# Borders between the stages of a two-layer diffusion block: order of the modulation rows, PSUM banks, and where two attention groups wait

## The chip, the core and the metric

The kernel runs on one NeuronCore of a Trainium2 chip. The metric is the device time of one execution in microseconds, the median of several runs. The engines are named as the profile names them: PE (TensorE; PEld is its weight load), DVE (VectorE), ACT (ScalarE), POOL (GpSimd), SP (SyncE, which issues nearly all DMAs here). Each engine takes its instructions in program order and waits at the head of its own queue for semaphores of others. PSUM has eight banks of 128 x 512 fp32.

## What is computed

Two transformer layers over 512 latent tokens (x) and 256 context tokens (ctx), width 1024. Every normalised input is scaled and shifted by modulation rows that come from a conditioning vector, `silu(c) @ ada_w`: nine rows of 1024 for each layer and stream. Shortened from the reference:

```python
for i in range(2):
    mx = (silu(c) @ ada_w[i] + ada_b[i]).reshape(B, 9, 1, D)      # of x
    mc = (silu(c_ctx) @ ada_w[i] + ada_b[i]).reshape(9, D)        # of ctx
    fx = swiglu(pre(hx, norm_w[i, 0], mx[:, 0], mx[:, 1]), w_gate[i, 0], w_up[i, 0], w_down[i, 0])
    hx = hx + 0.5 * mx[:, 2] * fx                                 # the same for hc
    ax, ac = pre(hx, norm_w[i, 1], mx[:, 3], mx[:, 4]), pre(hc, norm_w[i, 1], mc[3], mc[4])
    ox, oc = gqa_window(ax, ac) if i == 0 else diff_attn(ax, ac)  # each ends in "@ w_out"
    hx = hx + mx[:, 5] * ox
    fx = swiglu(pre(hx, norm_w[i, 2], mx[:, 6], mx[:, 7]), w_gate[i, 1], w_up[i, 1], w_down[i, 1])
    hx = hx + 0.5 * mx[:, 8] * fx
return rmsnorm(hx, final_norm_w)                                   # pre(h, w, shift, scale) = rmsnorm(h, w) * (1 + scale) + shift
```

## The kernel before

**Layout and stages.** Activations are kept transposed: the 1024 channels are 8 blocks `d` of 128 partitions, the 768 tokens (256 ctx, then 512 x) lie along the free dimension. `hT` (128 x 8 x 768) is the residual stream. `run` goes through six stages: `ffn(0,0)`, `gqa`, `ffn(0,1)`, `ffn(1,0)`, `diff`, `ffn(1,1)`; the last needs x alone.

**fp32 by three products.** Every operand is split into a rounded part and a rest. `weights` loads a 128 x 1024 weight tile into `w_raw` (a ring of four buffers), casts it on ACT into `w_hi` (L55) and subtracts on POOL into `w_lo` (L56; two buffers each). A product is then three matmuls: hi by hi, hi by lo, lo by hi.

**Ending a stage.** The last projection of a stage makes block `d` after block `d` of 128 channels in PSUM. As each is done, `residual` (DVE, L302) adds it to `hT`, once for ctx (256 columns) and once for x (512). The callback `after(d)` is then `x_block`: ACT writes the scaled copy `xh` (L184), DVE the rest `xl` (L185), ACT squares (`sq`, L194 and L197), and POOL adds the squares up in `acc` (L199; DVE for the last block). That makes the next stage's input while PE still projects.

**Starting a stage.** `ffn` opens the pool `pbig` of four double-bank tiles called `big` and projects the first gate and up blocks at once (`project_k`, L257): for each k of the 8 channel blocks six matmuls, k by k, so that block k of `xh` and `xl` is needed only at step k. The norm factor is applied afterwards. `projected` copies two bias columns from PSUM (DVE, L262). The attentions start in the same way with `project_halves` (L276), in two single-bank tiles.

**Modulation rows.** A `side` list of `ada_block`s (load a 128 x 1024 tile into `w_raw`, multiply it on DVE by the conditioning vector with an accumulating L131, once per stream) is worked off by `more()`: one block in each `up_block` and some in the down-projection. They feed a later stage. Their `ada_junk` output has one buffer.

**What sets the order.** The code is traced once; a scheduler then places each instruction on its engine's queue as soon as its inputs look ready, so code that is written later can stand earlier in a queue. A pool of tiles hands out its buffers in a ring; where a pool is opened over memory that another one had, each new tile waits for the last users of just the tiles that lay there.

**Attention outputs.** In `gqa`, `values(g, pp, qb)` makes the output of group g (of 4) and query block qb (of 6), 128 x 2 x 128. It is split into `oh` (ACT, L482) and the rest `o1` (POOL, L483) and both are written to the DRAM tensor `od` (in the profile `god`, L484 and L485). `load_o` reads a group back as `og` (L491). Groups 0 and 1 go through the first half of the out-projection while groups 2 and 3 are still attended to (`out_proj(0, ...)`); `out_proj(1, ...)` is the second half, with `after`. `diff` does the same with eight heads: heads 0 to 3 first, then `out_proj(1, ...)` over heads 4 to 7 (`o4` to `o7`, L727 to L729), whose last one never leaves the chip. `out_proj` takes units of two blocks; for the units (0, 1) it first adds up the groups or heads that are ready and then the late ones.

## Time and profile before

| | |
|---|---|
| median of 3 runs | 2881.77 us (2878.62 to 2882.25) |
| the profiled execution, own time | 2884.58 us |
| its span from the first to the last instruction | 2882.8 us |
| PE busy | 2765.0 us (96%) |
| PEld / DVE / POOL / ACT busy | 90% / 53% / 44% / 33% |
| mean granted TensorE clock | 0.988 of full |
| HBM | 275.63 MB, 96 GB/s over the span |

PE is busy for all but 118 us of the span. So a number that matters for the end is one in which PE waits, or in which it runs at a lower clock: the granted clock stands at 1.0 or at 0.5 (2.4 or 1.2 GHz), and the mean over a stretch tells what part of it was at half. A timeline row gives start and duration in us, engine, line, operation, output and inputs, shape, how many like it were merged, and in brackets how long the engine had been idle just before and who released it.

### The profile page before, as it was taken

The page shows a single profiled execution, that of the slowest core. Times are in us where ns is not written, and L with a number is a line of the kernel's source. Part 1 is how long each engine was busy: PE and PEld are TensorE (multiplying, and loading weights), DVE is VectorE, ACT ScalarE, POOL GpSimd, SP SyncE. Part 2 cuts the span into 40 slices and gives each one's busy share as a digit, 9 for nine tenths or more (in the row PEclk, how much of TensorE's full clock was granted, in tenths as well). Part 3 has the DMA queues.
Part 4 walks back from the last instruction along what each step waited for, and adds up shares of the span by engine and source line. Part 5 has one row for each costly group of instructions (what it writes and reads, how often), then busy time and mean ns, then how long its engine had stood idle before and what let it go on. Part 6 is the DMA issues. An engine that isn't in the chain of part 4 may idle for free. (4 is left out here: it accounts for less than half of the span.)

```text
span 2882.8 us, 40921 instructions
## 1 busy us (share of the span) xinstructions
PE 2765.0 (96%) x16162; PEld 2583.7 (90%) x16162; DVE 1523.9 (53%) x2661; ACT 962.3 (33%) x1727; POOL 1274.4 (44%) x750
## 2 busy tenths in 40 slices
...
GB/s 277 104 126 100 134 123 95 113 146 90 65 135 112 81 75 116 81 92 121 88 81 103 77 118 87 86 121 93 82 94 77 88 93 111 88 91 100 103 103 45
DMA packets 113567, 296.38 MB, mean 103 GB/s; under 512 B 13024, under 2 KB 31072, under 8 KB 113376
## 3 DMA queue, kind: packets, MB, share of 16 engines
...
q8 instruction: 128, 2.10, 0.3%
...
## 5 line engine op out<-in xcount | busy, mean ns | idle before, releaser
L56 POOL TENSOR_TENSOR w_lo<-w_raw,w_hi 128x1024 fp32r<-128x1024 f32 (+2 forms) x377 | 799.8, 2122 | 1114.2 <-ACT w_hi L55 1091.7
L55 ACT CAST w_hi<-w_raw 128x1024 fp32r<-128x1024 f32 (+2 forms) x377 | 337.5, 895 | 1142.4 <-PE big L70 398.1
L257 PE MATMUL big<-xh,w_hi 128*128 128x384 f32 (+3 forms) x2816 | 691.9, 327 | 22.4 <-DVE hT L302 13.1
L257 PE MATMUL big<-xl,w_hi 128*128 128x384 f32 (+3 forms) x2816 | 689.4, 326 | 3.3 <-DVE xl L185 3.2
L257 PE MATMUL big<-xh,w_lo 128*128 128x384 f32 (+3 forms) x2816 | 690.9, 327 | 0.4 <-POOL w_lo L56 0.4
L257 PEld LDWEIGHTS big<-xh,w_hi 128*128 128x128 f32 x2816 | 501.0, 191 | 26.7 <-ACT sq L197 11.1
L257 PEld LDWEIGHTS big<-xl,w_hi 128*128 128x128 f32 x2816 | 498.7, 190 | 4.1 <-DVE xl L185 4.1
L257 PEld LDWEIGHTS big<-xh,w_lo 128*128 128x128 f32 x2816 | 496.9, 190 | 0.8 <-POOL w_lo L56 0.8
L131 DVE SCALAR_TENSOR_TENSOR ada_junk<-w_raw,s_bc 128x1024 f32<-128x1024 f32 x224 | 330.1, 1474 | 304.5 <-DMA w_raw<-ada_w 302.3
L262 DVE COPY bias<-big 128x2 f32<-128x2 f32 x176 | 27.7, 158 | 629.3 <-PE big L257 629.2
L68 PE MATMUL big<-hh,w_hi 128*128 128x512 f32 (+1 forms) x1200 | 327.6, 344 | 0.0
L70 PE MATMUL big<-hl,w_hi 128*128 128x512 f32 (+1 forms) x1200 | 326.9, 343 | 0.0
L72 PE MATMUL big<-hh,w_lo 128*128 128x512 f32 (+1 forms) x1200 | 326.8, 344 | 0.0
L302 DVE SCALAR_TENSOR_TENSOR hT<-big,mod,hT 128x512 f32<-128x512 f32 (+1 forms) x288 | 167.9, 618 | 179.4 <-PE big L72 179.0
L70 PEld LDWEIGHTS big<-hl,w_hi 128*128 128x128 f32 x1200 | 225.6, 188 | 30.1
L72 PEld LDWEIGHTS big<-hh,w_lo 128*128 128x128 f32 x1200 | 224.7, 188 | 28.8 <-POOL w_lo L56 0.2
L68 PEld LDWEIGHTS big<-hh,w_hi 128*128 128x128 f32 x1200 | 224.8, 188 | 27.4
L969 POOL TENSOR_TENSOR hl<-tb,hh 128x768 fp32r<-128x768 f32 (+1 forms) x88 | 151.3, 1719 | 171.8 <-ACT hh L968 170.6
L964 DVE SCALAR_TENSOR_TENSOR tb<-tb,bias,ta 128x512 f32<-128x512 f32 (+1 forms) x154 | 176.2, 1177 | 8.3 <-DVE tb L295 0.5
L276 PE MATMUL half<-xh,w_hi 128*128 128x384 f32 (+3 forms) x464 | 154.6, 333 | 21.0 <-DVE ta L288 19.1
L968 ACT CAST hh<-tb 128x768 fp32r<-128x768 f32 (+1 forms) x88 | 68.7, 781 | 268.2 <-DVE tb L964 268.1
L276 PE MATMUL half<-xl,w_hi 128*128 128x384 f32 (+3 forms) x464 | 153.1, 330 | 0.0
...
## 6 DMA issues: line engine op xcount, KB each, us to landing
w_raw<-ffn_gu SPq DMA_DIRECT2D x176, 512.0 KB, 3.3
w_raw<-ada_w SPq DMA_DIRECT2D x128, 512.0 KB, 3.3
...
w_raw<-diff_in SPq DMA_DIRECT2D x24, 512.0 KB, 3.3
w_raw<-gqa_in SPq DMA_DIRECT2D x12, 512.0 KB, 3.5
...
ada_raw<-ada_w SPq DMA_DIRECT2D x8, 512.0 KB, 9.4
```

The source lines that it names most:

```text
L55: nc.scalar.copy(out=hi[:, :cols], in_=raw[:, :cols])
L56: nc.gpsimd.tensor_tensor(out=lo[:, :cols], in0=raw[:, :cols], in1=hi[:, :cols].bitcast(F32), op=ALU.subtract)
L68: nc.tensor.matmul(o, wh, xh, start=(k == 0), stop=False)
L70: nc.tensor.matmul(o, wh, xl, start=False, stop=False)
L72: nc.tensor.matmul(o, wl, xh, start=False, stop=(k == n - 1))
L131: getattr(nc, engines[s]).scalar_tensor_tensor(out=junk, in0=raw, scalar=1.0, in1=self.sbc[:, s], op0=ALU.mult, op1=ALU.mult, accum_out=se ...
L257: mm(ps[:, c, :e - s], w[:, k], x[:, k, s:e], start=first, stop=last)
L276: mm(ps[:, :e - s], w_[:, k], x[:, k, s:e], start=(k == 0 and i == 0), stop=(k == ND - 1 and i == 2))
L302: self.nc.vector.scalar_tensor_tensor(out=h, in0=o, scalar=self.mv(l, s, c, d), in1=h, op0=ALU.mult, op1=ALU.add)
L964: nc.vector.scalar_tensor_tensor(out=u[:, tk], in0=u[:, tk], scalar=bu[:, s:s + 1], in1=g[:, tk], op0=ALU.add, op1=ALU.mult)
L968: nc.scalar.copy(out=hh[:, toks], in_=u[:, toks])
L969: nc.gpsimd.tensor_tensor(out=hl[:, toks], in0=u[:, toks], in1=hh[:, toks].bitcast(F32), op=ALU.subtract)
```

## The change

Three things are changed, all of them where one stage ends and the next begins.

- **Modulation rows.** `projected` keeps the bias copy (L262) as `bias_copy`. While the index of the current block is 0, that is in the first `up_block` of the three `ffn` after the first one, `more()` runs inside `issue_after(self.bias_copy)`: what the `ada_block` puts on DVE is queued behind that copy, so behind the end of the first projection. Later blocks follow, since `ada_junk` has one buffer. DMAs on SP are not bound by it. `ffn(1,1)` has no such rows, so two stages are touched: `ffn(0,1)` and `ffn(1,0)`.
- **PSUM banks.** The out-projections of `gqa` and `diff` take some blocks from a pool `pfirst` of two banks which lies lowest (`gqa`: blocks 0 and 4, `diff`: blocks 0 and 1) and the rest from six banks; and `diff` opens its pools in the opposite order. In the built program the first `big` tile of `ffn(0,1)` has banks 0 and 1. Before, bank 0 was block 4's and bank 1 the 512 x tokens of block 7, the last one; now both were block 4's. The first tile of `diff` had bank 4, which the last block of `ffn(1,0)` had; now it has bank 0, block 4's, and its second half bank 3, block 6's. The first `big` tile of `ffn(1,1)` had bank 0 of block 6 and bank 1 of block 5; now blocks 0 and 1.
- **Groups 2 and 3 of `gqa`.** Their outputs are written straight into on-chip tiles: group 2 into `og2`, group 3 into four buffers of the query ring `qs` that are free by then. 24 stores, 8 loads and the DRAM space of two groups are gone. The split of a group 3 output is two ACT copies and two POOL subtractions of 128 x 128 in place of one each of 128 x 256. The pool `gqa_q` is opened earlier, so that it can be released later.

```diff
@@ -259,7 +259,7 @@
     def projected(self, ps, xonly=False):
         n = 256 if xonly else 384
         bias = self.sp.tile([P, 2], F32, name="bias")
-        self.nc.vector.tensor_copy(out=bias, in_=ps[:, 1, n:n + 2])
+        self.bias_copy = self.nc.vector.tensor_copy(out=bias, in_=ps[:, 1, n:n + 2]).ins
         return ps[:, :, :n], bias
 
     def project_halves(self, src, xonly=False, pool=None, tag="half"):
...
         sinks = lp.tile([P, 16], F32, name="sinks")
         nsink = lp.tile([P, 16], F32, name="nsink")
-        od = self.dp.tile([4, 2, P, 2, T], F32, name="god")
+        od = self.dp.tile([2, 2, P, 2, T], F32, name="god")
         self.hp.release()
         o2p = self.sb("gqa_o2", 1)
+        rq = self.sb("gqa_q", 8)
         rpp = self.sb("gqa_p", 8)
         rp = self.sb("gqa_r", 2)
         rt = self.sb("gqa_t", 3)
         rk = self.sb("gqa_k", 3)
-        rq = self.sb("gqa_q", 8)
         self.pbig = self.ps("pgqa", 1)
         ptr = self.ps("pgqa_t", 2)
...
             nc.vector.tensor_tensor(out=o1[0:64], in0=av[0:64, 0:256], in1=o2[0:64], op=ALU.add)
             nc.vector.tensor_tensor(out=o1[64:128], in0=av[64:128, 256:512], in1=o2[64:128], op=ALU.add)
             qc = slice(CTX + qb * P, CTX + (qb + 1) * P) if qb < 4 else slice((qb - 4) * P, (qb - 3) * P)
-            oh = rp.tile([P, 256], F32R, name="oh")
-            nc.scalar.copy(out=oh, in_=o1)
-            nc.gpsimd.tensor_tensor(out=o1, in0=o1, in1=oh.bitcast(F32), op=ALU.subtract)
-            nc.sync.dma_start(od[g, 0][:, :, qc], oh.bitcast(F32).rearrange("p (c n) -> p c n", c=2))
-            nc.sync.dma_start(od[g, 1][:, :, qc], o1.rearrange("p (c n) -> p c n", c=2))
+            o1 = o1.rearrange("p (c n) -> p c n", c=2)
+            if g < 2:
+                oh = rp.tile([P, 2, P], F32R, name="oh")
+                nc.scalar.copy(out=oh, in_=o1)
+                nc.gpsimd.tensor_tensor(out=o1, in0=o1, in1=oh.bitcast(F32), op=ALU.subtract)
+                nc.sync.dma_start(od[g, 0][:, :, qc], oh.bitcast(F32))
+                nc.sync.dma_start(od[g, 1][:, :, qc], o1)
+            elif g == 2:
+                oh = o2t[:, 0, :, qc]
+                nc.scalar.copy(out=oh, in_=o1)
+                nc.gpsimd.tensor_tensor(out=o2t[:, 1, :, qc], in0=o1, in1=oh.bitcast(F32), op=ALU.subtract)
+            else:
+                for c in range(2):
+                    oh = o3t[c][:, qc]
+                    nc.scalar.copy(out=oh, in_=o1[:, c])
+                    nc.gpsimd.tensor_tensor(out=o3t[2 + c][:, qc], in0=o1[:, c], in1=oh.bitcast(F32), op=ALU.subtract)
 
         def load_o(pool, g):
             t = pool.tile([P, 2, 2, T], F32R, name=f"og{g}")
-            for tk in (slice(0, T),) if g < 3 else (slice(CTX, 512), slice(512, T), CT):
-                for c in range(2):
-                    nc.sync.dma_start(t[:, c, :, tk].bitcast(F32), od[g, c][:, :, tk])
-            return t
...
-        def out_proj(pr, os_, units, after=None):
+            for c in range(2):
+                nc.sync.dma_start(t[:, c].bitcast(F32), od[g, c])
+            return part(t)
+
+        def part(t):
+
+            return lambda c, r: t[:, c, r]
+
+        def out_proj(pr, os_, units, after=None, first_banks=None):
 
             mm = nc.tensor.matmul
             cuts = ((1, CT), (0, XT))
@@ -499,7 +513,8 @@
             for u in units:
                 w = self.weights(a["gqa_out"][pr, u])
                 for i in range(2):
-                    todo.append((u * 2 + i, i, w, [self.pbig.tile([P, 512], F32, name="half")[:, :tk.stop - tk.start]
+                    pool = first_banks if first_banks and u * 2 + i in (0, 4) else self.pbig
+                    todo.append((u * 2 + i, i, w, [pool.tile([P, 512], F32, name="half")[:, :tk.stop - tk.start]
                                                    for s, tk in cuts]))
             for part in (((0, 1, 2, 3),) if len(units) == 1 else ((0, 1), (2, 3))):
...
@@ -508,12 +523,14 @@
                         for w, c, first, last in ((wh, 0, r == 0, False), (wh, 1, False, False),
                                                   (wl, 0, False, r == 3)):
                             for ps, (s, tk) in zip(outs, cuts):
-                                mm(ps, w[:, i * 4 + r], o[:, c, r % 2, tk], start=first, stop=last)
+                                mm(ps, w[:, i * 4 + r], o(c, r % 2)[:, tk], start=first, stop=last)
                     if part[-1] == 3:
                         self.residual(outs, cuts, 0, 5, d)
                         if after:
                             after(d)
...
                 o01 = self.sb("gqa_o", 1, side="right")
                 os_ = [load_o(o01, 0), load_o(o01, 1)]
-                o2 = load_o(o2p, 2)
+
+                o3t = [rq.tile([P, T], F32R, name="qs") for _ in range(4)]
             nxt = step(i + 1) if i < 23 else None
             other(i)
             values(g, pp, qb)
             pp = nxt
         o01.release()
-        rq.release(); rk.release(); rt.release(); rp.release(); rpp.release()
+        rk.release(); rt.release(); rp.release(); rpp.release()
         pss.release(); pav.release(); ptr.release(); self.pbig.release()
-        o3p = self.sb("gqa_o3", 1)
-        os_ = [o2, load_o(o3p, 3)]
+        os_ = [part(o2t), lambda c, r: o3t[2 * c + r]]
         self.x_open()
         self.x_bias(0, 2)
-        self.pbig = self.ps("pgqa_o", 8)
-        out_proj(1, os_, (0, 1), after)
-        for u in (2, 3):
-            out_proj(1, os_, (u,), after)
-        self.pbig.release()
-        o3p.release(); o2p.release()
+
+        pfirst = self.ps("pgqa_f", 2)
+        self.pbig = self.ps("pgqa_o", 6)
+        for units in ((0, 1), (2,), (3,)):
+            out_proj(1, os_, units, after, pfirst)
+        self.pbig.release(); pfirst.release()
+        rq.release(); o2p.release()
         lp.release()
 
 
     def diff(self, after):
         nc, a = self.nc, self.a
-        self.pbig = self.ps("pdiff", 1)
+        pss = self.ps("pdiff_s", 4)
         ptr = self.ps("pdiff_t", 2)
         pav = self.ps("pdiff_v", 1)
-        pss = self.ps("pdiff_s", 4)
+        self.pbig = self.ps("pdiff", 1)
         lp = self.sb("diff", 1)
         kp = self.sb("diff_k", 4)
...
@@ -713,13 +731,14 @@
                 nc.sync.dma_start(od[h, 0], oh.bitcast(F32))
                 nc.sync.dma_start(flat(od[h, 1]), r0)
 
-        def out_proj(pr, os_, units, pool, tag, after=None):
+        def out_proj(pr, os_, units, pool, tag, after=None, first_banks=None):
 
             mm = nc.tensor.matmul
             todo = []
             for u in units:
                 w = self.weights(a["diff_out"][pr, u])
-                todo += [(u * 2 + i, i, w, pool.tile([P, 512], F32, name=tag)) for i in range(2)]
+                todo += [(u * 2 + i, i, w, (first_banks if first_banks and u == 0 else pool).tile([P, 512], F32, name=tag))
+                         for i in range(2)]
             for part in (((0, 1, 2, 3),) if len(units) == 1 else ((0, 1, 2), (3,))):
                 for d, i, (wh, wl), ps in todo:
...
@@ -754,9 +773,10 @@
             if h < 7:
                 ks, qs, vv = new["k"], new["q"], new["v"]
         op.release(); vp.release(); pp.release(); p1p.release(); kp.release()
-        pss.release(); pav.release(); ptr.release(); self.pbig.release()
+        self.pbig.release(); pav.release(); ptr.release(); pss.release()
 
         op = self.sb("diff_oall", 1)
+        pfirst = self.ps("pdiff_f", 2)
         po = self.ps("pdiff_o", 6)
         self.x_bias(1, 2, True)
...
             os_.append((o[:, 0], o[:, 1]))
         os_.append((o7[:, 0], o7[:, 1]))
         for units in ((0, 1), (2,), (3,)):
-            out_proj(1, os_, units, po, "o", after)
-        po.release()
+            out_proj(1, os_, units, po, "o", after, pfirst)
+        po.release(); pfirst.release()
         op.release()
         lp.release()
...
         todo = list(side)
 
         def more(n=1):
-            for _ in range(n):
-                if todo:
-                    self.ada_block(self.adap, *todo.pop(0))
+
+            with self.tc.issue_after(self.bias_copy) if i == 0 and not first else nullcontext():
+                for _ in range(n):
+                    if todo:
+                        self.ada_block(self.adap, *todo.pop(0))
 
         if first:
```

The DVE queue at the border from `gqa` to `ffn(0,1)`, before, for the last block: its residuals `hT`, its rests `xl`, and what stands between them and the first two bias copies.

```order
L302 SCALAR_TENSOR_TENSOR hT<-half,mod,hT 128x256
L302 SCALAR_TENSOR_TENSOR hT<-half,mod,hT 128x512
L185 SCALAR_TENSOR_TENSOR xl<-hT,mod,xh 128x256
L185 SCALAR_TENSOR_TENSOR xl<-hT,mod,xh 128x512
L131 SCALAR_TENSOR_TENSOR ada_junk,mod<-w_raw,s_bc 128x1024
L199 TENSOR_TENSOR acc<-sq,acc 128x768
L131 SCALAR_TENSOR_TENSOR ada_junk,mod<-w_raw,s_bc 128x1024
L262 COPY bias<-big 128x2 x2
```

Two of the six modulation rows `ada_junk` stand ahead of the bias copies here; the other four stand higher up, among the rests of the blocks before. The same stretch now:

```order
L302 SCALAR_TENSOR_TENSOR hT<-half,mod,hT 128x256
L302 SCALAR_TENSOR_TENSOR hT<-half,mod,hT 128x512
L185 SCALAR_TENSOR_TENSOR xl<-hT,mod,xh 128x256
L185 SCALAR_TENSOR_TENSOR xl<-hT,mod,xh 128x512
L199 TENSOR_TENSOR acc<-sq,acc 128x768
L262 COPY bias<-big 128x2
L131 SCALAR_TENSOR_TENSOR ada_junk,mod<-w_raw,s_bc 128x1024 x5
L262 COPY bias<-big 128x2
L131 SCALAR_TENSOR_TENSOR ada_junk,mod<-w_raw,s_bc 128x1024
L210 TENSOR_SCALAR tb<-big 128x768
```

The six rows ahead of the first bias copy are behind it: five between the two bias copies, one after the second, ahead of the norm factor (`tb`, `rstd`). At the border from `ffn(0,1)` to `ffn(1,0)` it is the same with its six rows.

The SP queue at the end of `gqa` before, `og_8655` being group 3 and `og_7822` group 2:

```order
L485 DMA god<-o_8464 256x1x128
L491 DMA og_8655<-god 128x2x256 x3
L484 DMA god<-oh 256x1x128
L491 DMA og_8655<-god 128x2x256
L485 DMA god<-o_8597 256x1x128
L120 DMA s_bc<-cond 128x1024 x2
L484 DMA god<-oh 256x1x128
L485 DMA god<-o_8631 256x1x128
L491 DMA og_8655<-god 128x2x256 x2
L126 DMA w_raw<-ada_w 128x1024
```

Six loads and the last five stores of group 3 stand ahead of the first load of a modulation row (`ada_w`) here. And now, from the last load of group 1 on:

```order
L501 DMA og_7802<-god 128x1536 x2
L54 DMA w_raw<-gqa_out 128x1024 x2
L54 DMA w_raw<-ffn_gu 128x1024 x2
L120 DMA s_bc<-cond 128x1024 x2
L126 DMA w_raw<-ada_w 128x1024
```

The loads and stores of groups 2 and 3 are gone; the weight loads are next to each other.

The PE queue at the end of `diff`, before: the value products `av` of the last head, its sum of squares (L699) and then the first out-projection products of heads 4 to 6 (`o_21694` is head 4).

```order
L691 MATMUL av<-pth,vl 128x512
L692 MATMUL av<-ptl,vh 128x512
L690 MATMUL av<-pth,vh 128x512
L691 MATMUL av<-pth,vl 128x512
L692 MATMUL av<-ptl,vh 128x512
L699 MATMUL tr<-acc,ones 128x512
L727 MATMUL o<-o_21694,w_hi 128x512
L728 MATMUL o<-o_21694,w_hi 128x512
```

All products of the out-projection stand behind the value products and the sum of squares. Now some of them (L746 to L748, head 4 is `o_21668`, head 6 `o_21674`) stand ahead of that, here amid the value products:

```order
L710 MATMUL av<-ptl,vh 128x512
L708 MATMUL av<-pth,vh 128x512
L709 MATMUL av<-pth,vl 128x512
L710 MATMUL av<-ptl,vh 128x512
L746 MATMUL o<-o_21674,w_hi 128x512 x2
L708 MATMUL av<-pth,vh 128x512
L709 MATMUL av<-pth,vl 128x512
L747 MATMUL o<-o_21674,w_hi 128x512
L748 MATMUL o<-o_21674,w_lo 128x512
L747 MATMUL o<-o_21674,w_hi 128x512
L748 MATMUL o<-o_21674,w_lo 128x512
L710 MATMUL av<-ptl,vh 128x512
```

Of the 36 products of heads 4 to 6 for blocks 0 to 3, the 18 of blocks 0 and 1 moved ahead of the last head's sum of squares; behind it, 18 are left.

## Rows read from the trace of the kernel before

**Rows 1.** Stretches: length, PE, PEld, DVE, ACT, POOL busy (instructions), clock, DMA.
```profile
core 0: us, PE busy (x) PEld busy (x) DVE busy (x) ACT busy (x) POOL busy (x), PEclk, DMA share, GB/s
932.05:959.50 27.45, 27.45 (x142) 23.67 (x143) 22.44 (x27) 12.92 (x20) 12.89 (x6) 0.91 0.18 59
...
1531.20:1552.00 20.80, 15.45 (x65) 14.02 (x64) 17.29 (x21) 5.92 (x8) 8.20 (x4) 0.75 0.29 102
```
**Rows 2.** Timeline of PE, end of `gqa`: start, length, instruction, count, idle before.
```profile
932.05 1.76 PE L511 MATMUL half<-og,w_hi 128*128 128x256 f32 x4 [5.14 <-DMA og<-god]
...
970.79 0.98 PE L257 MATMUL big<-xh,w_hi 128*128 128x384 f32 x2 [10.76 <-DVE hT L302]
```
**Rows 3.** Timeline of POOL and SP's queue, last group 3 output and its load.
```profile
920.78 0.75 POOL L483 TENSOR_TENSOR o<-o,oh 128x256 f32<-128x256 f32 x1 [2.36 <-DMA og<-god]
...
928.89 1.23 SPq L491 DMA_DIRECT2D og<-god  x2
```
**Rows 4.** Groups of DVE and POOL, 932.05 to 974.7: count, busy, mean ns, idle before.
```profile
L185 DVE SCALAR_TENSOR_TENSOR xl<-hT,mod,xh 128x256 fp32r<-128x256 f32 (+1 forms) x16 | 23.3, 1481 | 0.7 <-ACT xh L184 0.7
L302 DVE SCALAR_TENSOR_TENSOR hT<-half,mod,hT 128x256 f32<-128x256 f32 (+1 forms) x16 | 9.3, 608 | 16.8 <-PE half L511 16.8
L131 DVE SCALAR_TENSOR_TENSOR ada_junk<-w_raw,s_bc 128x1024 f32<-128x1024 f32 x4 | 6.0, 1499 | 0.0
...
L199 POOL TENSOR_TENSOR acc<-sq,acc 128x768 f32<-128x768 f32 x6 | 13.4, 2227 | 4.8 <-PE half L511 3.8 <-ACT sq L197 1.0
L56 POOL TENSOR_TENSOR w_lo<-w_raw,w_hi 128x1024 fp32r<-128x1024 f32 x4 | 10.0, 2507 | 24.6 <-ACT w_hi L55 24.6
```
**Rows 5.** Timeline of DVE, from the first residual to the second bias copy.
```profile
935.98 1.18 DVE L302 SCALAR_TENSOR_TENSOR hT<-half,mod,hT 128x256 f32<-128x256 f32 x2 [15.77 <-PE half L511]
...
970.91 3.78 DVE L185 SCALAR_TENSOR_TENSOR xl<-hT,mod,xh 128x256 fp32r<-128x256 f32 x2 [0.27 <-ACT xh L184]
...
989.71 0.16 DVE L262 COPY bias<-big 128x2 f32<-128x2 f32 x1 [8.31 <-PE big L257]
```
**Rows 6.** Timeline of PE and DVE, border from `ffn(0,1)` to `ffn(1,0)`.
```profile
1531.22 0.51 PE L257 MATMUL big<-xh,w_hi 128*128 128x384 f32 x2
...
1541.33 1.01 PE L257 MATMUL big<-xl,w_hi 128*128 128x384 f32 x2 [3.22 <-DVE xl L185]
...
1545.08 1.01 PE L257 MATMUL big<-xh,w_hi 128*128 128x384 f32 x2 [2.10 <-ACT xh L184]
...
1545.32 0.75 DVE L185 SCALAR_TENSOR_TENSOR xl<-hT,mod,xh 128x512 fp32r<-128x512 f32 x1
```
**Rows 7.** Group of DVE's modulation rows, 1525.2 to 1546.1.
```profile
L131 DVE SCALAR_TENSOR_TENSOR ada_junk<-w_raw,s_bc 128x1024 f32<-128x1024 f32 x4 | 7.8, 1962 | 1.6 <-DMA w_raw<-ada_w 1.6
```
**Rows 8.** Timeline of PE, ACT and DVE, border from `ffn(1,0)` to `diff`.
```profile
2104.05 0.41 PE L276 MATMUL s<-xh,w_hi 128*128 128x384 f32 x1 [4.73 <-DVE hT L302]
...
2104.75 0.71 ACT L184 ACTIVATE xh<-hT,mod 128x512 fp32r<-128x512 f32 x1
...
2106.15 0.74 DVE L185 SCALAR_TENSOR_TENSOR xl<-hT,mod,xh 128x512 fp32r<-128x512 f32 x1
...
2114.11 1.45 PE L239 MATMUL s<-acc,ones 128*128 128x384 f32 x4
```
**Rows 9.** Timeline of PE and ACT, end of `diff`.
```profile
2462.09 0.39 PE L728 MATMUL o<-o,w_hi 128*128 128x512 f32 x1
...
2467.92 0.40 PE L729 MATMUL o<-o,w_lo 128*128 128x512 f32 x1
...
2469.41 0.73 ACT L709 ACTIVATE o<-hT,subw 128x512 fp32r<-128x512 f32 x1 [5.58 <-DVE hT L707]
2469.43 0.50 PE L727 MATMUL o<-o,w_hi 128*128 128x512 f32 x1 [1.12 <-DVE hT L707]
...
2489.49 0.48 PE L257 MATMUL big<-xh,w_hi 128*128 128x256 f32 x2 [2.39 <-DVE hT L302]
```
**Rows 10.** DMA issues on the page: count, KB each, median us to landing.
```profile
w_raw<-ffn_gu SPq DMA_DIRECT2D x176, 512.0 KB, 3.3
```

4 lines of the change are left out of this document (3 added, 1 removed).

## Prediction

> **What bounds the kernel now.** I read the engine shares first, then the granted clock by stretches, then the waits of PE by the line that ended them, and only then the timelines around those waits. PE is busy for 2765.0 of the span's 2882.8 us. Nothing can be gained but from the 118 us in which it idles and from stretches in which its clock stands at half. Both lie close together at the four borders that the change touches. At the first, PE waits 5.14 us for a DMA and 39 us later 10.76 us for a residual [rows 2]; the 27.45 us of unbroken work between have a mean clock of 0.91 [rows 1]. At the second, two waits of 3.22 and 2.10 us [rows 6] in a stretch of mean clock 0.75 [rows 1]. At the third, one of 4.73 us [rows 8]; at the fourth 1.12 and 2.39 us [rows 9]. In both stretches of [rows 1] the half clock stands behind or around PE's idle time, so a wait is paid twice: once as idle time, once as slow work.
>
> All sums are made in the profiled execution: 2884.58 us, its span 2882.8, 2.81 above the median of 2881.77. I apply the saving to the median.
>
> **A1: end of `gqa`, groups on chip.** The wait of 5.14 us at 932.05 [rows 2] is the end of a chain: POOL writes the last rest at 920.78 + 0.75 = 921.53, it is stored, and SP issues the loads of group 3 at 928.89 [rows 3]. PE had come to that place at 932.05 - 5.14 = 926.91. With the outputs on chip, the data is there when POOL is done. Two pieces of half the size cost a little more than one, which I set at 0.5 us: ready at about 922, with 4.9 us to spare. No wait takes its place. Behind it, 27.45 us ran at 0.91: (1 - 0.91) x 2 x 27.45 = 4.9 us of that at half clock, which lose 2.5. Without the wait I take PE to stay at full clock. A1 = 5.14 + 2.5 = 7.6 us. Inside `gqa`, 12 stores and 2 loads of group 2 and the splits of group 3 in two pieces move a few instructions; no wait of PE hangs on these stores, and ACT and POOL have slack (33% and 44% busy). I take 0, with 1.5 either way.
>
> **A2: first projection of `ffn(0,1)`.** PE's out-projection ended at 970.79 - 10.76 = 960.03 and would now, by 27.45 - 2.5 = 25.0 us of work (plus 0.5 for the gaps between), end at 926.9 + 25.5 = 952.4. The wait of 10.76 us is for a residual: block 7's, whose bank the first `big` tile was to take. With banks 0 and 1 both block 4's, that goes. What is late next is the input itself: the last `xl` of block 7, on DVE. From the first residual to the end of the last `xl`, DVE took 970.91 + 3.78 - 935.98 = 38.7 us [rows 5]. In that stand four modulation rows of 6.0 us, with 0.3 of overhead [rows 4]; they are now behind the bias copy. That leaves 32.4. The chain began 935.98 - 932.05 = 3.9 us behind PE's second half at half clock [rows 2, 5], so 2.0 at full clock: at 928.9, so it ends at 961.3. The other way to add it, from the busy times of `xl`, residuals and idling [rows 4], 23.3 + 9.3 + 0.7 = 33.3, gives 962.2. I take 962.0. PE begins the projection at 952.4, and works k by k, so block 7 is needed only at its last eighth: DVE idled 8.31 us between the first two bias copies, and a copy takes 0.16 [rows 5], so the second projection, at full clock, took 8.47 us and the first ended at 981.24. Thus block 7 is wanted 7.4 us in, at 959.8, and a **new wait of 2.2 us** (1.5 to 2.4) stands where 10.76 stood. Before, the first projection ran from 970.79 to 981.24, 10.4 us in place of 8.47: 1.9 lost at half clock. A2 = 10.76 + 1.9 - 2.2 = 10.5 us.
>
> Here a rule can be set against the row. The mean `xl` took 1481 ns in this stretch [rows 4], twice what one of 512 columns takes alone elsewhere (0.74 and 0.75 [rows 6, 8]), while POOL ran ten instructions of 2.2 to 2.5 us. So something of POOL holds DVE, and I use the long duration. The Trainium skill (SBUF — State Buffer, "Who interferes with whom") says that a VectorE instruction with two SBUF inputs and a GpSimd instruction that reads SBUF exclude each other for whole instructions; the trace agrees in that `xl` has both forms. By it the sum would be that of rival 2 below, which is priced from the rows.
>
> **The modulation rows, where they go.** All six of this stage pass the first bias copy on DVE; five run between the two bias copies, where DVE idled 8.31 us [rows 5], at 1.5 us each [rows 4], 7.5 in all, and one ahead of the norm factor. That factor is wanted only when the first gate block is finished on other engines, and PE has its next projection in the other buffers. So I cost them at nothing on PE. Queued behind them are the second bias copy and the factor (late by some 1.5 us, read by the evictions of the `big` tiles). Their loads on SP aren't held, but each of them keeps a `w_raw` buffer until its row is done; SP and the weight loads behind wait for that. A weight load takes 3.3 us [rows 10], and weights for some four projections of about 8.5 us are under way, so there are some 34 us of cover. If that cover is gone, it is rival 4.
>
> **B: `ffn(0,1)` to `ffn(1,0)`.** Here the bank came in time; PE began at 1531.22 and waited 3.22 for `xl` and 2.10 for the `xh` of the last block [rows 6]. In 20.80 us at a mean of 0.75, 10.4 were at half clock [rows 1]; some 2.4 of these were idle, so 4.0 are lost on work. At stake are 3.22 + 2.10 + 4.0 = 9.3. The chain on DVE ended at 1545.32 + 0.75 = 1546.07 [rows 6]; without its four rows of 7.8, their wait of 1.6 for the loads and 0.3 around them [rows 7], at 1536.4. PE wants the last block at 1531.2 + 7.4 = 1538.6. That holds with 2.2 us to spare; one POOL subtraction in the way (2.5 [rows 4]) would use it up, so I leave a wait of 0.5. B = 8.8 us.
>
> **C: `ffn(1,0)` to `diff`.** No modulation rows stand here; only the bank changes. PE was free at 2104.05 - 4.73 = 2099.32 and waited for block 7's residual [rows 8], then did 48 matmuls to 2114.11, 10.06 us, where the same 48 took 8.47 at full clock [rows 5]: 1.6 lost at half. Now the first tile has block 4's bank and PE starts at 2099.3. It does 42 of 48 matmuls (7.4 us) before block 7 is needed, but the scheduler has put block 7's first ones after 27, and the queue is in order. Block 7's `xh` is ready at 2104.75 + 0.71 = 2105.46, its `xl` at 2106.15 + 0.74 = 2106.89 [rows 8]; the change moves neither. So PE does 27 matmuls (4.8 us, to 2104.1), waits 1.3, does 7 more and waits 0.2 for `xl`, and ends at about 2109.3 in place of 2114.1. C = 4.8; I take 4.5, as one of the new waits may bring half clock back. Bounds: 6.4 (wait and clock both gone) and 2.0 (half clock remains).
>
> **D: end of `diff`.** 18 of the 36 first products stand now ahead of the last head's sum of squares. One takes (2467.92 - 2462.09) / 25 = 0.233 us [rows 9], so they delay it by up to 4.2 us. Before, these products filled PE's time until the last head's output `o7` came, at 2469.41 + 0.73 = 2470.14; PE, after its wait of 1.12 at 2469.43 and nine more products, wanted it at 2471.6: 1.5 us of slack. Now `o7` comes at 2470.1 + about 3.0 (some of the 18 fill gaps amid the value products) = 2473.1, and PE, with 18 left, waits: 1.5 lost, and 0.5 for the next weights' casts behind. On the other side is the wait of 2.39 us for the bank of the first `big` tile [rows 9]: the bank is now free in time, but the last `xl` still comes about as late, so I credit 1.0. D = -1.0, between +2.4 and -4.2.
>
> **Sum.** 7.6 + 10.5 + 8.8 + 4.5 - 1.0 = 30.4 us, 1.05%: 2881.8 - 30.4 = **2851.4 us** (2854.2 for a profiled execution such as this one).
>
> **The rivals.**
>
> *1. The new waits vanish too.* If the chain on DVE, with no rows in it, also meets POOL less often, the projections start and run through: 7.6 + 12.7 + 9.3 + 6.4 = 36.0, so 2845.8. For it: an `xl` alone takes half its mean here. Against it: POOL's work is not removed, and now stands closer to the same `xl`.
>
> *2. POOL holds DVE all the way.* POOL has ten instructions in that stretch, 13.4 + 10.0 = 23.4 us [rows 4]. If each is waited out by an `xl`, the chain is 23.4 and sixteen `xl` at 0.6, 33.0 in place of 23.3: 9.7 us longer, so that the wait at A2 remains about as it was and half clock returns (1.9); B loses 4. The gain is 30.4 - 9.7 - 1.9 - 4 = 14.8: 2867.0. For it: the rows stood between many of the `xl`, and without them more of the `xl` meet a POOL instruction. Against it: in that stretch DVE already waited 16.8 us for PE [rows 4], which the shorter chain can use.
>
> *3. The banks don't come free as told.* If the first tiles still wait for the last block's residual, that residual comes before the last two `xl`, at 962.0 - 3.8 = 958.2, and PE waits 5.8 us from 952.4, with 1.9 at half clock: A2 gives 10.76 - 5.8 = 5.0. C gives nothing and D loses its credit: 7.6 + 5.0 + 8.8 - 2.0 = 19.4, 2862.4. Against it: the banks as the built program gives them.
>
> *4. Slower: the deferred rows hold the weight ring.* Four `w_raw` buffers serve both rows and weights. If the rows run late, each of four loads for weights waits for a row, then 3.3 for its transfer [rows 10] and 2.5 for its subtraction [rows 4], 5.8; four times in two stages, 46 us. Against the gain of 30 that is +16: 2898. It decides once a row ends later than the 34 us of cover, and at five of the eight waits (29 us) gain and loss cancel. Against it: DVE idles 8.31 us [rows 5] right where the rows go.
>
> **How the numbers follow.** Forecast 0.60, with its own range 2845 to 2859 from the bounds of C and D and the 1.5 in `gqa`; rival 1 0.12, rival 2 0.15, rival 3 0.04, rival 4 0.09, of which 0.05 with most of its waits and 0.04 near the point where they cancel the gain. The range reaches from 2843 (rival 1 with D's gain) to 2868 (rival 2); outside lies rival 4, with the ends of the others. The bound of 0.2%, 5.8 us, is about what a measurement of this kernel can tell from no change. All cases but rival 4 are faster by more: 0.91 faster, 0.04 the same, 0.05 slower.
>
> **What would show it.** Right: no DMA wait at the first second-half product of `gqa` (L526) and a clock of 1.0 behind it; at the first projection of `ffn(0,1)` one wait of 2 us, on `xl` and not on `hT`; no `ada_junk` ahead of the bias copies; under 1 us at B; at C waits of about 1.3 us on block 7's `xh`; at D a wait of 2 to 3 us for `o7` (L746). Wrong: a mean `xl` above 1.9 us in that stretch (rival 2), a wait on `hT` at a projection's first matmul (rival 3), or waits of PE on weights in the first blocks of an `ffn` with SP behind an `ada_junk` (rival 4).

## The result, and the profile after

The changed kernel takes 2853.88 us (2852.81 to 2855.17), beside 2882.01 for the kernel before: a ratio of 0.9901, 95% interval 0.9889 to 0.9913, or 28.1 us less. The forecast was 2851.4. Measured again later, it took 2853.34 (ratio 0.9902, 0.9887 to 0.9917).

The profiled execution took 2853.44 us. From its page, the span and the engines:

```profile
span 2851.6 us, 40866 instructions
PE 2759.4 (97%) x16162; PEld 2578.0 (90%) x16162; DVE 1525.4 (53%) x2661; ACT 962.6 (34%) x1733; POOL 1279.3 (45%) x756
```

The span is 31.2 us shorter. PE's busy time fell by 5.6 of it, for the same 16162 products with less at half clock; the rest is idle time. Where it went is best read from PE's own milestones, the starts of the first and last products of each stage in the two timelines. "First projections" are here the 576 products of L257 with which an `ffn` begins, twelve projections in a row:

| stretch of PE | before | after | difference | forecast |
|---|---|---|---|---|
| start to first product of `gqa` | 606.73 | 606.01 | -0.7 | 0 |
| `gqa` to its last value product | 311.31 | 308.33 | -3.0 | 0 |
| A: on to the end of the first projections of `ffn(0,1)` | 157.30 | 136.91 | -20.4 | -18.1 |
| rest of `ffn(0,1)` | 455.88 | 455.58 | -0.3 | 0 |
| B: first projections of `ffn(1,0)` | 112.36 | 103.32 | -9.0 | -8.8 |
| rest of `ffn(1,0)` | 455.34 | 455.34 | 0 | 0 |
| C: last product of `ffn(1,0)` to `diff`'s first sum of squares | 15.18 | 10.68 | -4.5 | -4.5 |
| D: on to the end of the first projections of `ffn(1,1)` | 446.83 | 453.54 | +6.7 | +1.0 |
| rest | 312.02 | 312.11 | +0.1 | 0 |

The windows of the kernel after, with the columns of [rows 1]: the end of `gqa` up to the first projection, the border to `ffn(1,0)`, and the wait for the last head at the end of `diff`.

```profile
core 0: us, PE busy (x) PEld busy (x) DVE busy (x) ACT busy (x) POOL busy (x), PEclk, DMA share, GB/s
914.00:948.50 34.50, 34.50 (x197) 29.90 (x196) 23.38 (x28) 18.34 (x27) 17.36 (x11) 1.00 0.23 77
...
1504.00:1522.00 18.00, 17.73 (x100) 17.03 (x100) 16.29 (x18) 6.65 (x9) 11.44 (x5) 1.00 0.26 87
...
2430.00:2447.00 17.00, 12.65 (x39) 9.33 (x40) 5.50 (x7) 6.75 (x11) 7.22 (x6) 0.80 0.00 0
```

The first two had clocks of 0.91 and 0.75; both are at 1.00 now. In the third it is 0.80.

PE's timeline after, at the four borders (the last bracket is the idle time before, with its releaser):

```profile
948.47 0.52 PE L257 MATMUL big<-xh,w_hi 128*128 128x384 f32 x2
...
1506.84 0.52 PE L257 MATMUL big<-xh,w_hi 128*128 128x384 f32 x2
...
1507.97 0.62 PE L257 MATMUL big<-xh,w_lo 128*128 128x384 f32 x2 [0.27 <-POOL w_lo L56]
...
2066.98 0.45 PE L276 MATMUL s<-xh,w_lo 128*128 128x384 f32 x1 [0.74 <-POOL w_lo L56]
...
2072.13 0.62 PE L276 MATMUL s<-xh,w_hi 128*128 128x384 f32 x2 [0.47 <-ACT xh L184]
...
2430.40 1.12 PE L717 MATMUL tr<-acc,ones 128*128 128x512 f32 x2 [0.69 <-ACT acc L715]
...
2439.66 2.08 PE L746 MATMUL o<-o,w_hi 128*128 128x512 f32 x4 [3.95 <-ACT o L727]
...
2446.30 0.49 PE L746 MATMUL o<-o,w_hi 128*128 128x512 f32 x1
...
2463.19 0.51 PE L257 MATMUL big<-xl,w_hi 128*128 128x256 f32 x2 [0.87 <-DVE xl L185]
...
2471.27 1.12 PE L226 MATMUL big<-acc,ones 128*128 128x512 f32 x2 [1.55 <-DVE acc L199]
```

The waits of 5.14 and 10.76 us [rows 2] have no successor at all: the first projection begins at 948.47 without a bracket and runs through. Of the 5.32 us at the second border [rows 6], 0.27 is left; of the 4.73 at the third [rows 8], 0.74 for a weight and 0.47 for block 7's `xh`. At the fourth a new wait of 3.95 us for `o7` (L727) stands where 1.12 stood [rows 9], and two small ones follow in the projection. In a second profile of the same kernel that wait is the same, and a wait for a weight's cast follows it:

```profile
2439.89 2.08 PE L746 MATMUL o<-o,w_hi 128*128 128x512 f32 x4 [3.95 <-ACT o L727]
...
2446.38 0.50 PE L746 MATMUL o<-o,w_hi 128*128 128x512 f32 x1 [0.87 <-ACT w_hi L55]
```

### The profile page after: what moved, and what is told of

It reads as the page before. It is cut to its first block, busy times and chain, and to the rows that moved or that the text cites. A ratio compares the mean times of both kernels' runs of the same rounds, so it can differ in the third digit from the quotient of the medians.

```text
span 2851.6 us, 40866 instructions
## 1 busy us (share of the span) xinstructions
PE 2759.4 (97%) x16162; PEld 2578.0 (90%) x16162; DVE 1525.4 (53%) x2661; ACT 962.6 (34%) x1733; POOL 1279.3 (45%) x756
## 5 line engine op out<-in xcount | busy, mean ns | idle before, releaser
L257 PE MATMUL big<-xh,w_hi 128*128 128x384 f32 (+3 forms) x2816 | 689.8, 326 | 6.5 <-DVE xh L174 3.2
L257 PE MATMUL big<-xh,w_lo 128*128 128x384 f32 (+3 forms) x2816 | 688.7, 326 | 0.6 <-POOL w_lo L56 0.5
L257 PE MATMUL big<-xl,w_hi 128*128 128x384 f32 (+3 forms) x2816 | 686.8, 325 | 0.9 <-DVE xl L185 0.9
L257 PEld LDWEIGHTS big<-xh,w_hi 128*128 128x128 f32 x2816 | 499.4, 190 | 10.0 <-DVE tb L210 3.7
L131 DVE SCALAR_TENSOR_TENSOR ada_junk<-w_raw,s_bc 128x1024 f32<-128x1024 f32 x224 | 337.4, 1506 | 305.9 <-DMA w_raw<-ada_w 303.7
L257 PEld LDWEIGHTS big<-xl,w_hi 128*128 128x128 f32 x2816 | 496.8, 190 | 1.1 <-DVE xl L185 1.1
L257 PEld LDWEIGHTS big<-xh,w_lo 128*128 128x128 f32 x2816 | 494.6, 189 | 1.6 <-POOL w_lo L56 1.6
L262 DVE COPY bias<-big 128x2 f32<-128x2 f32 x176 | 27.6, 157 | 597.0 <-PE big L257 596.9
```

The source lines that it names most:

```text
L131: getattr(nc, engines[s]).scalar_tensor_tensor(out=junk, in0=raw, scalar=1.0, in1=self.sbc[:, s], op0=ALU.mult, op1=ALU.mult, accum_out=se ...
L257: mm(ps[:, c, :e - s], w[:, k], x[:, k, s:e], start=first, stop=last)
```

## The experiments

Each is told by its edit against the kernel that it names; times are medians, ratios those to the kernel before, measured beside it. Stretches are those of the table.

### The end of `diff`: the hoisted products

Held back, against the changed kernel (`last_ss` is the last head's sum of squares on PE):

```diff
+                    with self.tc.issue_after(self.last_ss) if pr == 1 else nullcontext():
+                        for r in part: ...   # the three products
```

> The changed kernel, with the out-projection products of heads 4 to 6 queued behind the last head's sum of squares on PE; the banks stay as changed. Theory 1: the 18 hoisted products delayed the last head by their own 4.2 us, and PE's wait of 3.95 us for o7 and the 6.8 us at half clock behind it come from that alone. Then 36 products stand between the sum of squares and o7 again, the wait is under 1.2 us, the clock stays at 1.0 there, and from PE's last start on the first-half products (2408.18 in the changed kernel) to the first projection of ffn(1,1) it takes some 44 us, where it took 48.4 after and 46.5 before: 2853.9 - 4.4 = 2849.5 us. Theory 2: o7 comes late whatever stands ahead, and the half clock falls in any case; the 18 products then stand behind a wait of about 8 us and the time stays at 2852 to 2855.

Measured: 2848.31 us (2846.15 to 2850.05), ratio 0.9882 (0.9867 to 0.9897). And with the part undone:

```diff
-        pfirst = self.ps("pdiff_f", 2)
-            out_proj(1, os_, units, po, "o", after, pfirst)
+            out_proj(1, os_, units, po, "o", after)
```

> The changed kernel, with all blocks of diff's second out-projection in the one pool of six banks again. Theory 1 (the 18 products are the loss, the banks the gain): the products go back behind the sum of squares, the wait of 3.95 us goes, but the first tile of ffn(1,1) waits for a late block's residual, 2.4 us or more with half clock behind it: 2851 to 2854 us, little from the changed kernel. Theory 2 (this part of the change only costs): 2849.5 us, as with the products held back.

Measured: 2848.09 us (2847.45 to 2851.33), ratio 0.9881 (0.9868 to 0.9895). PE's waits at that place, first held back, then undone:

```profile
2424.76 1.12 PE L717 MATMUL tr<-acc,ones 128*128 128x512 f32 x2 [0.69 <-ACT acc L715]
...
2439.24 0.50 PE L747 MATMUL o<-o,w_hi 128*128 128x512 f32 x1 [0.89 <-ACT w_hi L55]
...
2456.14 0.51 PE L257 MATMUL big<-xl,w_hi 128*128 128x256 f32 x2 [0.85 <-DVE xl L185]
...
2464.23 1.12 PE L226 MATMUL big<-acc,ones 128*128 128x512 f32 x2 [1.58 <-DVE acc L199]
```

```profile
2426.15 1.12 PE L717 MATMUL tr<-acc,ones 128*128 128x512 f32 x2 [0.69 <-ACT acc L715]
...
2440.61 0.50 PE L746 MATMUL o<-o,w_hi 128*128 128x512 f32 x1 [0.88 <-ACT w_hi L55]
...
2452.86 0.48 PE L257 MATMUL big<-xh,w_hi 128*128 128x256 f32 x2 [1.76 <-DVE hT L302]
...
2465.59 1.12 PE L226 MATMUL big<-acc,ones 128*128 128x512 f32 x2 [0.96 <-DVE acc L199]
```

In both the wait of 3.95 us is gone, and what is left there is 0.9 for a weight's cast; no half clock falls behind it. Theory 1 of the first run holds for the products: 5.5 us, and D takes 446.65 us, beside 446.83 before and 453.54 in the changed kernel. Theory 1 of the second run was half right on the banks: undone, a wait of 1.76 for the residual comes back, but 1.58 and 0.85 for the last sum and the last `xl` fall to 0.96 and 0, so in time the two kernels are the same, as its theory 2 has it. With the products held back, the two first banks of `diff` gain nothing.

### The three parts at the end of `gqa`, each taken out

```diff
-            with self.tc.issue_after(self.bias_copy) if i == 0 and not first else nullcontext():
```

> The changed kernel with the modulation rows where the scheduler puts them, the rest as changed. Theory 1 (each row stands in the chain of xl that the first projection waits for): at ffn(0,1) the last xl comes 6.3 us later, PE waits about 6 us in the projection and loses 1.7 at half clock; at ffn(1,0) the waits of 3.22 and 2.10 come back with 4.0 at half clock, 9.1 in all: 2853.9 + 16.8 = 2870.7 us. Theory 2 (at ffn(0,1) the bank was the whole matter, and rows fill time in which DVE waits for PE): only 9.1 come back, 2863.

Measured: 2870.39 us (2869.23 to 2872.95), ratio 0.9959 (0.9946 to 0.9971). A is 8.4 us longer than in the changed kernel, B 8.3. PE's waits, at A and at B:

```profile
959.03 0.62 PE L257 MATMUL big<-xh,w_hi 128*128 128x384 f32 x2 [0.74 <-ACT xh L184]
...
960.86 0.61 PE L257 MATMUL big<-xl,w_hi 128*128 128x384 f32 x2 [1.22 <-DVE xl L185]
...
962.67 0.62 PE L257 MATMUL big<-xh,w_hi 128*128 128x384 f32 x2 [0.85 <-ACT xh L184]
...
965.59 1.01 PE L257 MATMUL big<-xl,w_hi 128*128 128x384 f32 x2 [2.30 <-DVE xl L185]
...
1528.96 0.62 PE L257 MATMUL big<-xl,w_hi 128*128 128x384 f32 x2 [3.22 <-DVE xl L185]
...
1532.71 1.01 PE L257 MATMUL big<-xh,w_hi 128*128 128x384 f32 x2 [2.79 <-ACT xh L184]
```

Theory 1, nearly to the number: 5.1 us of waits on `xh` and `xl` and a stretch at half clock at A, and at B the pair that stood before. The rows did stand in the chain.

```diff
-        pfirst = self.ps("pgqa_f", 2)
-        self.pbig = self.ps("pgqa_o", 6)
+        self.pbig = self.ps("pgqa_o", 8)
```

> The changed kernel with one pool of eight banks for gqa's second out-projection. Theory 1 (the bank is a wait of its own): the first big tile of ffn(0,1) waits for the residual of block 7, which ended about 952.3 in the changed kernel where PE was free at 948.5: 4 us of wait on hT, and 1.7 at half clock: 2853.9 + 5.7 = 2859.6 us. Theory 2 (with the chain earlier, the bank is free before PE asks): no change, 2854.

Measured: 2856.82 us (2853.35 to 2859.71), ratio 0.9909 (0.9895 to 0.9922). PE's wait at the first projection:

```profile
954.68 0.98 PE L257 MATMUL big<-xh,w_hi 128*128 128x384 f32 x2 [2.53 <-DVE hT L302]
```

The wait on `hT` is there, of 2.53 us in place of 4, with some 1.5 lost at half clock behind it: A is 4.1 us longer. The median rose by 2.9, between the theories, and the intervals of the two kernels overlap; the row shows the wait, the times alone would not.

### Each part alone, on the kernel before

> The kernel before, with the modulation rows queued behind the first bias copy, and nothing else of the change. Theory 1 (rows stand in the chain at both borders): at ffn(1,0) 9.1 us; at ffn(0,1) the last residual, whose bank PE waits for, comes up to 6.3 us earlier and the wait of 10.76 us falls to some 5: 2882 - 15 = 2867 us. Theory 2 (with gqa's groups still late, DVE waits for PE there, and the rows only filled that time): the wait stays above 9 us, and the time is 2882 - 9.1 = 2873.

Measured: 2864.53 us (2864.23 to 2869.41), ratio 0.9939 (0.9927 to 0.9951): the largest part. The interval is a gain of 14.1 to 21.0 us, which holds the 15 of theory 1 and not the 9.1 of theory 2; B alone is 9.3 us shorter. PE's waits at A:

```profile
933.07 1.70 PE L511 MATMUL half<-og,w_hi 128*128 128x256 f32 x4 [6.66 <-DMA og<-god]
...
962.82 0.59 PE L257 MATMUL big<-xh,w_hi 128*128 128x384 f32 x2 [2.52 <-DVE hT L302]
```

The DMA wait stays and is even longer, but the wait for the residual fell from 10.76 to 2.52, by 8.2 us where the rows take 6.0. Of the rest, 0.8 is PE coming later behind the longer DMA wait; what is left is in the `xl`, of which more below.

The edit of the next keeps only the on-chip groups, with one pool of eight banks:

```diff
+                oh = o2t[:, 0, :, qc]      # group 2; group 3 likewise into o3t
-        os_ = [o2, load_o(o3p, 3)]
+        os_ = [part(o2t), lambda c, r: o3t[2 * c + r]]
```

> The kernel before, with groups 2 and 3 of gqa kept on chip, and nothing else of the change: the rows stay in the chain, the banks are the old ones. Theory 1 (PE's DMA wait of 5.14 us and the half clock behind it fall away, and DVE's chain starts earlier by as much): the wait of 5.14 us is gone, 10 us or so remain at the first projection of ffn(0,1), and its start is 7.6 us earlier: 2882 - 8 = 2874 us, a little less if the 3.0 us that gqa's inside took less in the changed kernel come from here. Theory 2 (DVE's chain ends when it did, since it is bound by its own work): the wait at the first projection grows by what the other lost, and the time is 2880 to 2882.

Measured: 2875.51 us (2872.77 to 2877.65), ratio 0.9974 (0.9962 to 0.9985). PE's one wait at A:

```profile
960.17 0.98 PE L257 MATMUL big<-xh,w_hi 128*128 128x384 f32 x2 [9.24 <-DVE hT L302]
```

Theory 1: the DMA wait and its half clock are gone, and DVE's chain came earlier by nearly as much, so that 9.24 us remain.

> The kernel before, with gqa's second out-projection in two pools, two banks and six, and nothing else of the change. Theory 1 (the last xl, with rows in its chain, is late next): PE begins the first projection of ffn(0,1) 10.8 us earlier, but the last xl still ends at about 974.7 and block 7 is wanted 7.4 us after 960.0, so waits of about 7 us and the half clock stay: 3.5 us of gain, 2878.5. Theory 2 (the bank is the wait): 10 us or more of gain, 2872.

Measured: 2876.14 us (2873.75 to 2880.51), ratio 0.9977 (0.9968 to 0.9986), A 10.9 us shorter, some 2 of it given back inside `gqa` and at C. PE's waits:

```profile
923.17 1.16 PE L512 MATMUL half<-og,w_hi 128*128 128x512 f32 x5 [1.74 <-DMA og<-god]
...
962.28 0.61 PE L257 MATMUL big<-xh,w_hi 128*128 128x384 f32 x2 [0.77 <-ACT xh L184]
...
964.11 0.62 PE L257 MATMUL big<-xl,w_hi 128*128 128x384 f32 x2 [1.22 <-DVE xl L185]
...
965.53 1.01 PE L257 MATMUL big<-xh,w_hi 128*128 128x384 f32 x2 [0.45 <-ACT xh L184]
...
968.85 1.01 PE L257 MATMUL big<-xl,w_hi 128*128 128x384 f32 x2 [2.31 <-DVE xl L185]
```

Four waits on `xh` and `xl`, 4.75 us, take the place of one of 10.76 on `hT`, as theory 1 says. But the DMA wait also shrank, from 5.14 to 1.74: with other pools the scheduler found another order for the second out-projection (x columns first, 128x512 in the row where 128x256 stood), which no theory had. So the time lies between the two.

The three parts alone shorten A by 7.7, 8.3 and 10.9 us, 26.9 in all; together they give 20.4. Each takes away a piece of the same two waits.

### `diff`'s pools alone

```diff
-        self.pbig = self.ps("pdiff", 1)
+        pss = self.ps("pdiff_s", 4)
...
-        pss = self.ps("pdiff_s", 4)
+        self.pbig = self.ps("pdiff", 1)
```

> The kernel before, with diff's pools of PSUM opened in the opposite order, and nothing else of the change. Theory 1 (the bank of the first tile is all of the third border): the wait of 4.73 us and the half clock go, two waits under 1 us stay, 4.8 us; inside diff 1.3 to 1.9 us are lost, as in the changed kernel with the first banks undone; at its end 1.9 are won: 2882 - 5 = 2877 us. Theory 2 (the loss inside diff comes from where other stages end, by chance): 2882 - 6.7 = 2875. Both would be 2882 if block 7's xh were what PE waits for in any case.

Measured: 2876.12 us (2873.05 to 2881.6), ratio 0.9975 (0.9965 to 0.9985). PE's waits at C, the same pair as in the changed kernel:

```profile
2096.41 0.44 PE L276 MATMUL s<-xh,w_lo 128*128 128x384 f32 x1 [0.71 <-POOL w_lo L56]
...
2101.55 0.62 PE L276 MATMUL s<-xh,w_hi 128*128 128x384 f32 x2 [0.47 <-ACT xh L184]
```

C is 4.6 us shorter, where theory 1 had 4.8. From the last sum of squares of `diff` to the end of the first projections of `ffn(1,1)` this kernel takes 97.4 us; the kernel before takes 99.5, and so do the other three with the old pool order. These 2.1 us are the 1.9 that theory 1 had won at `diff`'s end. The time itself, 7.1 us less, lies between the theories and does not decide. Inside `diff`, up to the last sum of squares, this kernel took 350.3 us, the kernel before 347.3; but `rows_only`, with the old pools, took 349.8. Without the hoisted products the four kernels with the old order took 347.3 to 349.8, those with the new 348.6 to 350.3. A cost of the pool order of about 1 us is possible and not settled.

### What makes an `xl` slow

The adds of squares on POOL left out, against the changed kernel:

```diff
-            eng = nc.vector if d == ND - 1 else nc.gpsimd
-            eng.tensor_tensor(out=self.acc[:, toks], ...)
+            if d == ND - 1:
+                nc.vector.tensor_tensor(out=self.acc[:, toks], ...)
```

> The changed kernel, leaving out POOL's six adds of squares for each norm whose input is made while the stage before ends (the sum is then of two blocks only). Theory 1 (a slow xl is one that starts beside a POOL instruction and waits for its end): with six of eleven such instructions gone at the border from gqa to ffn(0,1), the mean xl falls from 1.26 to about 0.9 us and the last one ends 3 us or more earlier; since PE waits there no more, the time falls by under 3 us, to 2851 to 2854. Theory 2 (an xl is slow for a reason of its own, such as what ACT writes beside it): the mean stays above 1.15 us, and the last one ends where it did.

Measured: 2845.61 us (2843.79 to 2846.75). The groups of DVE and POOL at the end of `gqa`, 916 to 957 us, with the columns of [rows 4]; first the changed kernel, then this one:

```profile
L185 DVE SCALAR_TENSOR_TENSOR xl<-hT,mod,xh 128x512 fp32r<-128x512 f32 (+1 forms) x16 | 19.8, 1256 | 6.3 <-ACT xh L184 6.3
...
L302 DVE SCALAR_TENSOR_TENSOR hT<-half,mod,hT 128x512 f32<-128x512 f32 (+1 forms) x16 | 9.3, 608 | 5.2 <-PE half L526 5.2
...
L199 POOL TENSOR_TENSOR acc<-sq,acc 128x768 f32<-128x768 f32 x6 | 12.4, 2066 | 5.9 <-ACT sq L197 5.9
L56 POOL TENSOR_TENSOR w_lo<-w_raw,w_hi 128x1024 fp32r<-128x1024 f32 x4 | 10.3, 2576 | 11.5 <-ACT w_hi L55 11.5
```

```profile
L185 DVE SCALAR_TENSOR_TENSOR xl<-hT,mod,xh 128x512 fp32r<-128x512 f32 (+1 forms) x16 | 16.6, 1050 | 5.8 <-ACT xh L184 5.8
...
L56 POOL TENSOR_TENSOR w_lo<-w_raw,w_hi 128x1024 fp32r<-128x1024 f32 x4 | 9.7, 2430 | 24.4 <-ACT w_hi L55 24.4
```

The mean `xl` fell from 1256 to 1050 ns, not to the 900 expected, but below the 1150 of theory 2. Which ones are still slow settles it. DVE's and POOL's timelines of this kernel, at one subtraction:

```profile
934.65 0.74 DVE L185 SCALAR_TENSOR_TENSOR xl<-hT,mod,xh 128x512 fp32r<-128x512 f32 x1
935.56 3.05 DVE L185 SCALAR_TENSOR_TENSOR xl<-hT,mod,xh 128x256 fp32r<-128x256 f32 x2 [0.17 <-ACT xh L184]
```

```profile
935.19 2.47 POOL L56 TENSOR_TENSOR w_lo<-w_raw,w_hi 128x1024 fp32r<-128x1024 f32 x1 [3.90 <-ACT w_hi L55]
```

The `xl` that began at 934.65, ahead of the subtraction, took 0.74 us although it ran on beside it. The next began at 935.56, inside it; the row holds two `xl`, which together took 3.05, and the first of them ended at 937.94, 0.28 us after the subtraction. So it is in all four slow ones of this kernel and all nine of the changed one: each began inside a POOL instruction and ended 0.28 us (256 columns) or 0.55 (512) after the end of one. The Trainium skill (SBUF — State Buffer, "Who interferes with whom") says that whichever of the two is issued first has the shared ports for its whole instruction and the other is blocked; the trace agrees for the `xl`, by the 0.28 and 0.55 above.

That the time fell by 8 us, and not by under 3, no theory had. The stretches say where most of it is: C by 2.0, the first projections of `ffn(1,1)` by 3.0, and nothing at A, as expected. At these two places PE waited for what stands behind the adds: a weight's rest in POOL's own queue (0.74) and block 7's `xh` (0.47) at C, the last `xl` and the sum of squares at `ffn(1,1)` (0.87 and 1.55). The next run takes up that hint: products held back, and all adds on DVE.

```diff
-            eng = nc.vector if d == ND - 1 else nc.gpsimd
-            eng.tensor_tensor(out=self.acc[:, toks], ...)
+            nc.vector.tensor_tensor(out=self.acc[:, toks], ...)
```

> The changed kernel with diff's products held back as before, and in addition the adds of squares on DVE in place of POOL. Theory 1 (a POOL add costs the xl beside it some 1.3 us, an add on DVE 0.96 us for 768 columns and 0.69 for 512): DVE's chains keep their length within 2 us, the wait for the last sum at ffn(1,1) (1.6 us) falls, and the time is 2846 to 2849 us, 2848.3 being that of the products held back alone. Theory 2 (leaving the adds out gave 8 us by taking work off POOL, which holds the weights' rests): 2842 or less. Theory 3 (the adds lengthen DVE's chain by their own 5.8 us, and the last xl is late again at ffn(0,1)): 2853 or more.

Measured: 2844.78 us (2842.93 to 2847.16), ratio 0.9871 (0.9858 to 0.9885), the lowest median here, 8.6 us under the changed kernel measured beside it. Against the products held back alone (0.9882, 0.9867 to 0.9897) the 3.5 us are not clear of noise. Groups of DVE, 914 to 957 us (`hT`, not shown, as before):

```profile
L185 DVE SCALAR_TENSOR_TENSOR xl<-hT,mod,xh 128x512 fp32r<-128x512 f32 (+1 forms) x16 | 15.5, 985 | 2.7 <-ACT xh L184 2.7
...
L198 DVE TENSOR_TENSOR acc<-sq,acc 128x768 f32<-128x768 f32 x7 | 6.6, 949 | 1.1 <-ACT sq L197 1.1
```

Seven adds of 6.6 us came onto DVE, where one of 1.0 stood; the `xl` gave back 19.8 - 15.5 = 4.3 of these 5.6. The chain kept its length within 2 us, so theory 1 holds in its step. The median is 1.2 us below its range, and the lowest and highest times reach from 2842.93 into it, so a larger gain than it gave is not shown. What the trace does show is that at C both waits vanished (8.67 us in place of 10.36 with the products held back), while at `ffn(1,1)` one wait of 2.03 for the last `xl` takes the place of 0.85 and 1.58. Theory 3 is out: no wait at A.

### The changed kernel once more

> The changed kernel once more, beside the others of this call. Theory 1: 2853.9 us, and inside gqa and diff its segments differ from the first profile by up to 2 us, as they do between kernels that have these stages in common. Theory 2 (those segments belong to the kernel): they repeat within 0.5 us.

Measured: 2853.34 us (2852.35 to 2855.14). Its stretches repeat: `gqa` 308.05 (308.33 the first time), `diff` to the last sum of squares 354.68 (354.76). That speaks for theory 2. Against it, the kernels with `diff`'s products held back and with its first banks undone have the same PE order in `gqa`, and took 306.5 and 309.9 there. So it stays open what moves this stretch by 2 or 3 us. All the same, the kernels with the groups on chip took 306.5 to 309.9 us in it, and the four others 310.1 to 312.4.

## Where the forecast was right and where not

**A1 was right in kind and size.** From the last value product to the end of the out-projection PE took 970.79 - 10.76 - 918.04 = 41.99 us; now 948.47 - 914.34 = 34.13, 7.9 less for a forecast of 7.6, and the on-chip kernel alone, with 34.3, shows that it comes from there. The 3.0 us inside `gqa` were set at 0 and are double the bound of 1.5. The split into kernels with and without the groups on chip speaks for this part as their cause, but no row shows it, and the scatter among those with the groups on chip is as large.

**A2 was right that the bank was only the nearest wait and the chain the next, and wrong on the chain.** The new wait of 2.2 us did not come, and A2 gave 12.5 us for 10.5. PE was where the forecast had it: 34.1 us behind the last value product for 952.4 - 918.04 = 34.4. The last `xl` came earlier, 955.95 - 914.34 = 41.6 us behind that product for 962.0 - 918.04 = 44.0. The step that failed is the chain's length, 32.4 to 33.1 us: it kept the `xl` at 23.3 us with the rows taken out. They fell to 19.8, and to 18.5 with the rows alone removed; there the chain, begun as before, took 29.7 us (936.79 to 966.52), and as much with the rows and the groups changed but not the banks. The changed kernel's own chain is no measure of that, as it began early:

```profile
918.28 0.75 DVE L302 SCALAR_TENSOR_TENSOR hT<-half,mod,hT 128x512 f32<-128x512 f32 x1 [1.75 <-PE half L526]
...
954.38 1.57 DVE L185 SCALAR_TENSOR_TENSOR xl<-hT,mod,xh 128x512 fp32r<-128x512 f32 x1 [1.25 <-ACT xh L184]
```

Block 0's x columns go first here, 10.6 us ahead of the forecast's 928.9. They do so in every kernel with the two pools, also in the one with the pools alone, and in none with one pool, also not in the one with the groups alone: the order comes with the pools, and it does not bring the end forward (with the banks undone the first residual is at 928.63, and the last `xl` ends 40.5 us behind the last value product).

Sixteen `xl` alone would take 8 x (0.48 + 0.74) = 9.8. In all three kernels nine of the sixteen begin inside an instruction of POOL; the excess is 13.5 us before, 10.0 now and 8.7 with the rows alone removed, 1.5, 1.1 and 1.0 for each of the nine. So it isn't how often they meet POOL that changed, but how much of its instruction is still to come. The last `xl` ended at 955.95, when PE wanted it at 948.47 + 7.4 = 955.9: met to a tenth, so that no wait at all is left there is in part luck. So rival 1's outcome came true for A and B, without C, but not for its reason, fewer meetings with POOL. Rival 2 had the mechanism, which the runs show, with the wrong sign: without the rows the `xl` meet POOL as often and wait less.

**B and C were right**, B with 9.0 for 8.8, and 9.3 with the rows alone; C with 4.5 for 4.5, and 4.6 with the pools alone. At C the waits are 0.74 and 0.47 in place of 1.3 and 0.2, the first of them for a weight that the forecast did not have, and the clock stayed at 1.0.

**D was wrong in size, and outside its bounds.** It was to cost 1.0, at most 4.2, and cost 6.7. With the products held back D takes 446.65 us, beside 446.83 before, so it is they that cost. Three terms of the forecast failed. The hoisted products were to fill gaps and delay the sum of squares by 3.0; from the last wait in the first half to that sum it is 2430.40 - 2408.18 = 22.22 us now, 2460.89 - 2443.03 = 17.86 before, so they delayed it by 4.36 and filled nothing. The slack of 1.5 us that PE had ahead of `o7` held the bank wait of 1.12, which the same edit takes away: 4.36 - 0.4 gives the 3.95 measured. And no half clock was counted behind that wait: at a mean of 0.80 over 17 us (the window above), 6.8 were at half, 0.6 of them idle, and the products took 3.1 longer. What that costs in the end is not shown. In the second profile the mean over the same stretch is 0.90, so 3.4 us at half, and PE then waits 0.87 for a weight's cast; the product behind it begins 2446.38 - 2439.89 = 6.49 us after the end of the wait for `o7`, and the same one in the first profile 2446.30 - 2439.66 = 6.64 us after it. The credit of 1.0 for the first banks did not come: from the last sum of squares to the end of the first projections it is 97.4 us with the products held back and 97.4 without the first banks. Both are 2.1 below the kernel before, as the kernel with the pool order alone is, so what was won at this border comes with the order of `diff`'s pools. Ahead of all this, from the first sum of squares of `diff` to the last wait in the first half, the changed kernel took 332.0 us, the kernel before 328.9, for which the forecast had nothing. That stays open: with the old pool order that stretch takes 328.9 to 331.4, with the new 329.5 to 332.2.

**Rivals 3 and 4 did not show.** No first projection waits on `hT`, and the rest of `ffn(0,1)` and of `ffn(1,0)` is the same to 0.3 us: six rows behind the bias copy hold up no weight.

**The sum** was -30.4 for a profiled difference of -31.1, by errors that cancel: -3.0 inside `gqa` and -2.3 at A that it did not have, +5.7 at D. That it came within 1 us is luck; that B and C came out is not. The median moved by 28.1 only, as the profiled execution of before was 2.8 us above its median and that of after was not; applying a saving read in one execution to the median has such an error.
